# Moving gate products, a fourth sum and low parts from GpSimd to VectorE in a four-layer diffusion trunk

## The chip, the cores and the metric

The kernel runs on one core of a Trainium2 chip. Its engines run side by side, each through its own queue in order: TensorE (PE, and PEld for its weight loads) multiplies matrices into PSUM, VectorE (DVE) and ScalarE (ACT) read PSUM and SBUF, GpSimd (POOL) reads SBUF, and SyncE (SP) issues transfers. The metric is the time of one execution on the device in microseconds (us); the median of several executions counts.

## What is computed

Two layers of a trunk are applied to two groups of tokens, 128 of a context and 512 of a noisy latent. Each layer has three sub-layers: a SwiGLU, a mixer (a recurrent one in the first layer, a pooling one in the second) and another SwiGLU. All have the same frame, cut here to what matters:

```python
def _layer(x, mod, l, norm_g, ffn_w1, ffn_w3, ffn_w2, mixer):
    sh1, sc1, g1, sh2, sc2, g2, sh3, sc3, g3 = jnp.split(mod[:, None, :].astype(x.dtype), N_MOD, axis=-1)
    h = _modulate(_rmsnorm(x, norm_g[l, 0]), sh1, sc1)
    x = x + 0.5 * g1 * _rmsnorm(_swiglu(h, ffn_w1[l, 0], ffn_w3[l, 0], ffn_w2[l, 0]), norm_g[l, 1])
    h = _modulate(_rmsnorm(x, norm_g[l, 2]), sh2, sc2)
    y, st = mixer(h)
    x = x + g2 * _rmsnorm(y, norm_g[l, 3])
    h = _modulate(_rmsnorm(x, norm_g[l, 4]), sh3, sc3)
    x = x + 0.5 * g3 * _rmsnorm(_swiglu(h, ffn_w1[l, 1], ffn_w3[l, 1], ffn_w2[l, 1]), norm_g[l, 5])
    return x, st
```

with `_swiglu(x, w1, w3, w2) = (silu(x @ w1) * (x @ w3)) @ w2`, 1024 channels and 2816 hidden ones, all in float32.

## The kernel before

The 640 tokens lie as five tiles of 128: 0 to 3 are the latent, 4 is the context. A float32 operand of a product is split into a high part (a copy to a narrower type, on ScalarE) and a low part (the difference, a subtraction, on VectorE); three products of the parts give one (`split`, lines 218 to 220; the weights in `weight_gen`, L137 and L138, L178 and L181). The first matrices of a SwiGLU are multiplied by a scheme with seven products in place of eight: from the four quarters of the operand (A11, A12, A21, A22) it makes the sums S1 to S4 (`h_sums`), and the products take A11, A12, S2, S3, S1, A22 and S4 in that order, each with high and low part.

Where one sub-layer ends and the next begins, the kernel does the following for each of the five tiles (`close`):

- The last product of the old sub-layer is added to y, in two halves of 512 channels, n = 0 and 1 (L643, on VectorE, from PSUM; L1087 and L1089 after the pooling mixer).
- `res_half`: ScalarE sums the squares of the half (L385), and the half is then multiplied in place by the gate row G (L411), on VectorE for n = 1 of tiles 0 to 2 and on GpSimd for the rest. The product overwrites what the square reads, so it waits for it.
- `res_close`: VectorE adds up the squares (L379), GpSimd takes the power -1/2 (L381), and VectorE makes the residual x + y * power, in two halves (L419). `c_next` squares x on ScalarE, spills x through SP, takes another L379 and L381, and scales x on ScalarE (L431).
- `c_t`: TensorE transposes the scaled x (L505), ScalarE and VectorE apply the modulation to the transposed pieces (L516, L514). Ahead of the recurrent and the pooling mixer the result is split as it is (L219 high, L220 low). Ahead of a SwiGLU it feeds the quarters: tiles 0, 1 and half of tile 2 make A11 and A12, the other half of tile 2 and tiles 3 and 4 make A21 and A22, and with them the sums.
- `h_sums`: S1 (L464), S2 (L465), S3 (L468) on VectorE; S4 (L472) and the low part of A22 on GpSimd, named by `aside`; all high parts on ScalarE. Tile 2's halves of A11 and A12 are copied for later sums by GpSimd (L531).

There are six such places, which the text calls seams: after the first SwiGLU (to the recurrent mixer; around 475 to 530 us of the span), after the recurrent mixer (738 to 815), after the second SwiGLU (1200 to 1265), after the third (to the pooling mixer; 1678 to 1725), after the pooling mixer (1725 to 1815), and the end (2200 on), where x goes out instead of on. The sums are made after the second, third and fifth seam.

The order of TensorE's instructions is the program's own in most phases (`manual_schedule`); on the other engines a scheduler orders the instructions by priorities and by its own costs before the program runs, and that order is then fixed. Weights are loaded by SP, split some products ahead into a ring of buffers, and so their splits (L137, L138, L154 to L160, L178, L181) lie between the instructions of a seam.

Of the kernel before, what the change touches and what calls it, by code (L numbers as in the profile page):

```python
# [12 lines left out]
AF = mybir.ActivationFunctionType  # L13
ALU = mybir.AluOpType
# [19 lines left out]
HK = KC // 2  # L34
# [49 lines left out]
class Kern:  # L84
# [321 lines left out]
    def res_half(self, t, n, l, s):  # L406

        y = self.y[t][:, n * 512:(n + 1) * 512]
        v = 1 if t < NT - 1 else 0
        self.square(self.t("mhl", [P, 512], BF16), y, self.ms[t], n)  # L410
        (self.nc.vector if n and t < 3 else self.nc.gpsimd).tensor_tensor(y, y, self.G[(l, s)][:, v, n * 512:(n + 1) * 512], op=ALU.mult)  # L411

    def res_close(self, t):

# [60 lines left out]
    def c_t(self, tiles, l, s, plain, tag="q"):  # L475

        nc = self.nc
        ab = self.ab[(l, s)]
        t = tiles[0]
        v = 1 if t < NT - 1 else 0  # L480
        w = P * len(tiles)
        n = 512 // w
        sl = slice(t * P, t * P + w)
        second = None
        if not plain:
            if t * P + w <= HT:
                dst = lambda kk: self.F[0][kk // HK][:, kk % HK, sl]
            else:
                o = max(0, t * P - HT)
                sums = slice(o, (t + 1) * P - HT)  # L490
                if t * P < HT:
                    self.f2 = [self.view(self.t("g", [P, 2 * TOK])) for _ in range(4)]
                    hf = self.t("yacc", [P, D]).rearrange("p (k t) -> p k t", k=KC)
                    dst = lambda kk: hf[:, kk]
                    cut = HT - t * P
                    second = [hf[:, 0:HK, cut:P], hf[:, HK:KC, cut:P]] + [x[:, :, sums] for x in self.f2[2:]]
                else:
                    dst = lambda kk: self.f2[kk // HK][:, kk % HK, sums]
                    second = [x[:, :, sums] for x in self.f2]
                self.sums[t] = self.h_sums(slice(0, HK), sums, second, nc.gpsimd)  # L500
        for j in range(KC // n):
            pt = self.p(tag)
            for q in range(n):
                for i, tt in enumerate(tiles):
                    nc.tensor.transpose(pt[:, q * w + i * P:q * w + (i + 1) * P], self.y[tt][:, (j * n + q) * P:(j * n + q + 1) * P],  # L505
                                        self.col("ident"))
            if plain:
                hp = self.t("c", [P, n, w])
                dst = lambda kk: hp[:, kk % n]
            for q in range(n):  # L510
                kk = j * n + q
                sr = pt[:, q * w:(q + 1) * w]
                if j % 2:
                    nc.vector.tensor_scalar(dst(kk), sr, ab[:, 1, kk, v:v + 1], ab[:, 0, kk, v:v + 1], op0=ALU.mult, op1=ALU.add)  # L514
                else:
                    nc.scalar.activation(dst(kk), sr, AF.Identity, scale=ab[:, 1, kk, v:v + 1], bias=ab[:, 0, kk, v:v + 1])  # L516
            if plain:
                for q in range(0, n, 2):
                    k2 = (j * n + q) // 2
                    self.split(self.hh[k2][:, :, sl], self.hl[k2][:, :, sl], hp[:, q:q + 2])  # L520
        if plain:
            return
        if second is None:
            for j in range(2):
                self.h_first(j, slice(0, HK), sl)
        elif t * P < HT:
            own = slice(t * P, HT)
            for j, name in enumerate(("A11", "A12")):
                self.h_put(name, slice(0, HK), own, hf[:, j * HK:(j + 1) * HK, 0:cut])
            for j in range(2):  # L530
                nc.gpsimd.tensor_copy(self.F[0][j][:, :, own], hf[:, j * HK:(j + 1) * HK, 0:cut])  # L531


    def mmP(self, out, h, w, ks=range(HK), start=True, stop=True, first=0, last=HK - 1, onto=False):
# [837 lines left out]
```

## Time and profile before

| what | value |
|---|---|
| median of 3 runs | 2235.13 us (2234.14 to 2235.29) |
| profiled execution, its own time | 2239.17 us |
| its span in the trace | 2237.3 us |
| mean granted TensorE clock | 0.969 of full speed |
| busy: TensorE, VectorE, ScalarE, GpSimd | 2113.8, 1687.4, 1005.0, 169.3 us |

The profiled execution is one further execution, so times of the trace are counted against 2239.17 us and only differences are carried to the median. Starts in the trace are counted in us from the beginning of its span.

### The profile page before, as it was taken

The page shows a single profiled execution, that of the slowest core. Times are in us where ns is not written, and L with a number is a line of the kernel's source. Part 1 is how long each engine was busy: PE and PEld are TensorE (multiplying, and loading weights), DVE is VectorE, ACT ScalarE, POOL GpSimd, SP SyncE. Part 2 cuts the span into 40 slices and gives each one's busy share as a digit, 9 for nine tenths or more (in the row PEclk, how much of TensorE's full clock was granted, in tenths as well). Part 3 has the DMA queues.
Part 4 walks back from the last instruction along what each step waited for, and adds up shares of the span by engine and source line. Part 5 has one row for each costly group of instructions (what it writes and reads, how often), then busy time and mean ns, then how long its engine had stood idle before and what let it go on. Part 6 is the DMA issues. An engine that isn't in the chain of part 4 may idle for free.

```text
span 2237.3 us, 32900 instructions
## 1 busy us (share of the span) xinstructions
PE 2113.8 (94%) x13101; PEld 1916.7 (86%) x13101; DVE 1687.4 (75%) x2647; ACT 1005.0 (45%) x1733; POOL 169.3 (8%) x173
## 2 busy tenths in 40 slices
PE   6899999998898989999999899999997789999997
PEld 4798999987797778999998798988996779999997
DVE  5967777767978796777877977777776786787875
ACT  5443333357857654333335542332336754333332
POOL 0000000012201310000002200000002320000002
PEclk7999999998999999999999999999998989999999
DMA  8424422234424453432224434444434352222222
GB/s 278 169 99 151 151 76 95 76 113 132 137 95 151 151 177 104 153 130 73 86 76 151 170 110 144 152 152 146 155 104 142 112 185 85 76 94 75 77 75 94
DMA packets 72714, 278.26 MB, mean 124 GB/s; under 512 B 7393, under 2 KB 15601, under 8 KB 61297
## 3 DMA queue, kind: packets, MB, share of 16 engines
q1 hardware_dynamic: 72528, 276.16, 35.9%
q8 instruction: 102, 1.67, 0.3%
q14 instruction: 52, 0.42, 0.1%
q0 software_dynamic: 32, 0.01, 0.0%
HBM read 260.40 MB, written 15.74 MB: 123 GB/s over the span
## 4 chain that ended last, share of the span: by engine, by line
PE 78%; DVE 11%; ACT 5%; issue 2%; POOL 2%; DMA 2%; SPq 1%; POOLq 0%; DVEq 0%; ACTq 0%
PE q L540 40%; PE b L633 25%; PE b L540 6%; PE m L287 2%; PE q L549 2%; DVE h L220 2%; DVE mw L419 2%; POOL st L381 1%; DVE wp L138 1%; ACT yacc L431 1%; DMA raw<-in_w_dram 1%; DVE st L379 1%; DVE wp L181 1%; DVE h L926 1%; PE b L887 1%
## 5 line engine op out<-in xcount | busy, mean ns | idle before, releaser
L540 PE MATMUL q<-h,wp 128*128 128x320 f32 x6312 | 946.0, 311 | 15.1 <-ACT h L219 8.9
L540 PEld LDWEIGHTS q<-h,wp 128*128 128x128 f32 x6312 | 933.6, 189 | 30.5 <-ACT h L219 10.4
L633 PE MATMUL b<-wp,g 128*128 128x512 f32 x2880 | 672.0, 393 | 4.6 <-DVE g L220 2.6
L633 PEld LDWEIGHTS b<-wp,g 128*128 128x128 f32 x2880 | 540.4, 189 | 124.4 <-DVE g L220 4.3
L137 ACT ACTIVATE wp<-raw 128x512 fp32r<-128x512 f32 x430 | 263.1, 629 | 631.1 <-PE b L633 328.0
L643 DVE TENSOR_TENSOR yacc<-yacc,b 128x512 f32<-128x512 f32 x380 | 258.1, 685 | 140.4 <-PE b L633 139.3
L138 DVE TENSOR_TENSOR wp<-raw,wp 128x512 fp32r<-128x512 f32 x430 | 294.4, 692 | 82.8 <-ACT wp L137 80.7
L181 DVE TENSOR_TENSOR wp<-raw,wp 128x1024 fp32r<-128x1024 f32 x118 | 144.1, 1222 | 77.8 <-PE q L540 52.5
L540 PE MATMUL b<-h,wp 128*128 128x320 f32 x960 | 156.7, 322 | 24.9 <-ACT h L219 16.8
L540 PEld LDWEIGHTS b<-h,wp 128*128 128x128 f32 x960 | 147.5, 196 | 36.1 <-ACT h L219 18.8
L178 ACT ACTIVATE wp<-raw 128x1024 fp32r<-128x1024 f32 x94 | 99.6, 1059 | 162.4 <-PE q L540 143.8
L411 POOL TENSOR_TENSOR yacc<-yacc,G 128x512 f32<-128x512 f32 x42 | 58.6, 1401 | 1320.7 <-ACT mhl L385 1320.5
L137 ACT ACTIVATE wp<-T 128x512 fp32r<-128x512 f32 x176 | 105.1, 623 | 70.6 <-PE q L540 70.6
L154 DVE TENSOR_TENSOR T<-raw 128x1024 f32<-128x1024 f32 x88 | 107.6, 1223 | 37.9 <-DMA raw<-in_w_dram 36.8
L549 PE MATMUL q<-h,wp 128*128 128x320 f32 x768 | 123.5, 316 | 8.9 <-ACT h L219 6.6
L549 PEld LDWEIGHTS q<-h,wp 128*128 128x128 f32 x768 | 117.1, 193 | 13.2 <-ACT h L219 6.9
L138 DVE TENSOR_TENSOR wp<-T,wp 128x512 fp32r<-128x512 f32 x176 | 116.7, 687 | 10.3 <-ACT wp L137 10.0
L287 PE MATMUL m<-mw,csil 128*32 128x256 f32 x1024 | 72.6, 393 | 9.1 <-DMA mw<-in_mod_w_dram 9.1
L219 ACT ACTIVATE g<-c 128x1280 fp32r<-128x1280 f32 x44 | 56.2, 1278 | 43.1 <-DVE c L615 42.9
L220 DVE TENSOR_TENSOR g<-c,g 128x1280 fp32r<-128x1280 f32 x44 | 65.4, 1486 | 11.2 <-ACT g L219 11.1
L609 ACT ACTIVATE c<-c 128x960 f32<-128x960 f32 x44 | 44.0, 1000 | 47.3 <-DVE c L586 47.3
L160 DVE TENSOR_TENSOR raw<-raw 128x512 f32<-128x512 f32 x88 | 60.4, 686 | 1.1
(211 smaller groups left out, 1736.7 us busy)
## 6 DMA issues: line engine op xcount, KB each, us to landing
raw<-in_w_dram SPq DMA_DIRECT2D x88, 1024.0 KB, 4.8
mw<-in_mod_w_dram SPq DMA_DIRECT2D x130, 512.0 KB, 4.5
raw<-in_w_dram SPq DMA_DIRECT2D x88, 512.0 KB, 4.6
x_spill<-mw SPq DMA_DIRECT2D x25, 512.0 KB, 2.6
mw<-x_spill SPq DMA_DIRECT2D x25, 512.0 KB, 3.7
raw<-in_w_dram SPq DMA_DIRECT2D x32, 256.0 KB, 5.5
raw<-in_w_in_dram SPq DMA_DIRECT2D x16, 512.0 KB, 4.4
wp<-in_mod_w_dram SPq DMA_DIRECT2D x8, 512.0 KB, 9.7
```

The costliest lines, as they stand in the source:

```text
L137: parts = [nc.scalar.activation(w[:, 0:512], src, AF.Copy), V.tensor_sub(w[:, 512:D], src, w[:, 0:512].bitcast(F32))]
L138: V.tensor_sub(w[:, 512:D], src, w[:, 0:512].bitcast(F32))]
L154: V.tensor_sub(T, raw[:, 512:1536], raw[:, 0:1024])
L160: V.tensor_sub(t4, t2, b21)
L178: nc.scalar.activation(wh, r, AF.Copy)
L181: V.tensor_sub(wl, r, wh.bitcast(F32))
L220: (engine or self.nc.vector).tensor_tensor(lo, src, hi.bitcast(F32), op=ALU.subtract))
L287: nc.tensor.matmul(ps[32 * j:32 * j + 32, 0:256], self.csil[:, k, :], w[:, j * 256:(j + 1) * 256], start=(k == 0), stop=(k == KC - 1), til ...
L540: self.nc.tensor.matmul(out, a, b[:, k], start=(start and not onto and k == first and n == 0), stop=(stop and k == last and n == 2), skip_ ...
L549: self.nc.tensor.matmul(out, a[:, sl], b[k // 2][:, k % 2, cols], start=(n == 0), stop=(n == 3 * KC - 1))
L633: nc.tensor.matmul(pb, a[:, ts_], b[:, ns], start=(c == 0), stop=(c == total - 1))
L643: nc.vector.tensor_add(y, y, pb)
```

## The change

Three lines change. In `res_half` the gate products stay on GpSimd only for n = 0 of tiles 0 and 1; before, GpSimd had n = 0 of all tiles and n = 1 of tiles 3 and 4. So 12 of the 60 products of the program are left on GpSimd, where there were 42. In `c_t` the sums are made without `aside`, so that S4 and the low part of A22 go to VectorE, and the two copies of tile 2 go to ScalarE.

```diff
@@ -408,7 +408,7 @@
         y = self.y[t][:, n * 512:(n + 1) * 512]
         v = 1 if t < NT - 1 else 0
         self.square(self.t("mhl", [P, 512], BF16), y, self.ms[t], n)
-        (self.nc.vector if n and t < 3 else self.nc.gpsimd).tensor_tensor(y, y, self.G[(l, s)][:, v, n * 512:(n + 1) * 512], op=ALU.mult)
+        (self.nc.vector if n or t > 1 else self.nc.gpsimd).tensor_tensor(y, y, self.G[(l, s)][:, v, n * 512:(n + 1) * 512], op=ALU.mult)
 
     def res_close(self, t):
 
@@ -497,7 +497,7 @@
                 else:
                     dst = lambda kk: self.f2[kk // HK][:, kk % HK, sums]
                     second = [x[:, :, sums] for x in self.f2]
-                self.sums[t] = self.h_sums(slice(0, HK), sums, second, nc.gpsimd)
+                self.sums[t] = self.h_sums(slice(0, HK), sums, second)
         for j in range(KC // n):
             pt = self.p(tag)
             for q in range(n):
@@ -528,7 +528,7 @@
             for j, name in enumerate(("A11", "A12")):
                 self.h_put(name, slice(0, HK), own, hf[:, j * HK:(j + 1) * HK, 0:cut])
             for j in range(2):
-                nc.gpsimd.tensor_copy(self.F[0][j][:, :, own], hf[:, j * HK:(j + 1) * HK, 0:cut])
+                nc.scalar.activation(self.F[0][j][:, :, own], hf[:, j * HK:(j + 1) * HK, 0:cut], AF.Copy)
```

The scheduler also orders VectorE's and ScalarE's instructions anew around the moved ones. Three places on VectorE show it.

The first is the end of the sums of the third seam, from tile 4's S2 on, before the change. `h_11016` is the low part of S2, `h_11018` of S3, `h_11020` of S1 and `h_11022` of S4; `wp` are weights of later products.

```order
L220 TENSOR_TENSOR h_11020<-g_11298,h_11019 128x4x128
L220 TENSOR_TENSOR h_11022<-c_11026,h_11021 128x4x128
L220 TENSOR_TENSOR h_11016<-g_11299,h_11015 128x4x128
L468 TENSOR_TENSOR c_11025<-c_11025,g_11296 128x4x128
L220 TENSOR_TENSOR h_11020<-g_11298,h_11019 128x4x128
L220 TENSOR_TENSOR h_11022<-c_11026,h_11021 128x4x128
L220 TENSOR_TENSOR h_11018<-c_11025,h_11017 128x4x128
L138 TENSOR_TENSOR wp_11576<-T_11570,wp_11576 128x512
```

The same place of the changed program, on the same engine, with `h_11024` for the low part of A22 and `c_11026` for S4:

```order
L220 TENSOR_TENSOR h_11016<-g_11299,h_11015 128x4x128
L220 TENSOR_TENSOR h_11024<-g_11297,h_11023 128x4x128
L472 TENSOR_TENSOR c_11026<-c_11026,g_11299 128x4x128
L468 TENSOR_TENSOR c_11025<-c_11025,g_11296 128x4x128
L220 TENSOR_TENSOR h_11020<-g_11298,h_11019 128x4x128
L220 TENSOR_TENSOR h_11022<-c_11026,h_11021 128x4x128
L220 TENSOR_TENSOR h_11018<-c_11025,h_11017 128x4x128
L220 TENSOR_TENSOR h_11024<-g_11297,h_11023 128x4x128
L472 TENSOR_TENSOR c_11026<-c_11026,g_11299 128x4x128
L156 TENSOR_TENSOR raw_11331<-raw_11331,T_11570 128x512
L573 TENSOR_TENSOR c_11553<-b_11555,yacc_11325 128x320
L220 TENSOR_TENSOR h_11022<-c_11026,h_11021 128x4x128
```

L472 and A22's low parts now stand between VectorE's own instructions; S2's last low part has five instructions between it and S3's last where it had three, and S4's last comes after all others.

The second place is tile 3 in the first seam (`yacc_1085` is its y, `yacc_1086` tile 4's, `mw_4436` its x).

```order
 L220 TENSOR_TENSOR h_4349<-c_4543,h_4345 128x2x256
 L643 TENSOR_TENSOR yacc_1086<-yacc_1086,b_4579 128x512
+L411 TENSOR_TENSOR yacc_1085<-yacc_1085,G_1435 128x512 x2
+L379 SCALAR_TENSOR_TENSOR st_4489<-st_4489 128x1
 L220 TENSOR_TENSOR h_4350<-c_4553,h_4346 128x2x256
-L379 SCALAR_TENSOR_TENSOR st_4489<-st_4489 128x1
-L181 TENSOR_TENSOR wp_4660<-raw_4216,wp_4315 128x1024
 L419 SCALAR_TENSOR_TENSOR mw_4436<-yacc_1085,st_4525,mw_4436 128x512 x2
 L220 TENSOR_TENSOR h_4351<-c_4563,h_4347 128x2x256
```

Both products of tile 3 now stand one behind the other in VectorE's queue, with the sum of squares behind them, and the weight split L181 that stood ahead of the residual has gone further back.

The third place is the end of the program (`yacc_17055`, `yacc_17056` and `yacc_17057` are y of tiles 2, 3 and 4).

```order
+L411 TENSOR_TENSOR yacc_17056<-yacc_17056,G_17275 128x512
 L643 TENSOR_TENSOR yacc_17056<-yacc_17056,b_20321 128x512
+L411 TENSOR_TENSOR yacc_17056<-yacc_17056,G_17275 128x512
 L379 SCALAR_TENSOR_TENSOR st_20303<-st_20303 128x1
+L643 TENSOR_TENSOR yacc_17057<-yacc_17057,b_20345 128x512
 L419 SCALAR_TENSOR_TENSOR mw_20258<-yacc_17056,st_20339,mw_20258 128x512 x2
-L643 TENSOR_TENSOR yacc_17057<-yacc_17057,b_20345 128x512
+L411 TENSOR_TENSOR yacc_17057<-yacc_17057,G_17275 128x512
 L643 TENSOR_TENSOR yacc_17057<-yacc_17057,b_20362 128x512
+L411 TENSOR_TENSOR yacc_17057<-yacc_17057,G_17275 128x512
 L379 SCALAR_TENSOR_TENSOR st_20344<-st_20344 128x1
 L419 SCALAR_TENSOR_TENSOR mw_20301<-yacc_17057,st_20380,mw_20301 128x512 x2
```

Each half is now added, multiplied, and only then is the next half added, and tile 4's first add has moved ahead of tile 3's residual.

## Rows read from the trace of the kernel before

**Rows 1.** The page: busy time by engine, and TensorE's 40 slices in tenths.
```profile
PE 2113.8 (94%) x13101; PEld 1916.7 (86%) x13101; DVE 1687.4 (75%) x2647; ACT 1005.0 (45%) x1733; POOL 169.3 (8%) x173
...
PE   6899999998898989999999899999997789999997
```

**Rows 2.** Five seams: stretch, length, busy PE, PEld, DVE, ACT, POOL; clock, DMA.
```profile
470.00:530.00 60.00, 49.06 (x245) 41.70 (x244) 42.23 (x76) 37.09 (x88) 17.80 (x20) 0.89 0.42 140
735.00:815.00 80.00, 70.62 (x418) 61.08 (x417) 66.58 (x113) 50.74 (x112) 26.02 (x26) 0.94 0.43 150
1195.00:1265.00 70.00, 56.75 (x320) 49.56 (x319) 62.43 (x100) 46.19 (x106) 27.99 (x25) 0.93 0.39 136
1675.00:1725.00 50.00, 39.13 (x210) 33.92 (x210) 32.45 (x57) 31.78 (x76) 16.25 (x17) 0.90 0.49 158
1725.00:1815.00 90.00, 68.20 (x405) 62.58 (x406) 66.40 (x119) 61.87 (x145) 33.58 (x25) 0.84 0.32 106
```

**Rows 3.** Timeline of TensorE: start, duration, instructions, idle time before and its releaser.
```profile
509.08 0.90 PE L549 MATMUL q<-h,wp 128*128 128x320 f32 x2 [6.62 <-ACT h L219]
...
797.82 5.39 PE L540 MATMUL b<-h,wp 128*128 128x320 f32 x35 [0.73 <-DVE h L220]
...
1253.62 0.64 PE L540 MATMUL b<-h,wp 128*128 128x320 f32 x1 [5.86 <-ACT h L219]
1257.24 8.42 PE L540 MATMUL b<-h,wp 128*128 128x320 f32 x47 [2.99 <-DVE h L220]
...
1811.06 8.21 PE L540 MATMUL b<-h,wp 128*128 128x320 f32 x36 [3.85 <-ACT h L219]
```

**Rows 4.** One line, the gate products L411: min/median/max in ns by engine.
```profile
L411 POOL TENSOR_TENSOR yacc<-yacc,G x42: 1262/1292/2123, 478.7 to 2230.3; 128x512 f32<-128x512 f32 x42
...
L411 DVE TENSOR_TENSOR yacc<-yacc,G x18: 678/686/1139, 480.6 to 2219.1; 128x512 f32<-128x512 f32 x18
```

**Rows 5.** Timelines of GpSimd and VectorE, first seam; then line L379 as in rows 4.
```profile
500.55 2.95 POOL L411 TENSOR_TENSOR yacc<-yacc,G 128x512 f32<-128x512 f32 x2 [2.06 <-ACT mhl L385]
...
502.30 1.23 DVE L379 SCALAR_TENSOR_TENSOR st<-st 128x1 f32<-128x1 f32 x1
...
505.10 1.41 DVE L419 SCALAR_TENSOR_TENSOR mw<-yacc,st,mw 128x512 f32<-128x512 f32 x2 [0.44 <-POOL st L381]
...
L379 DVE SCALAR_TENSOR_TENSOR st<-st x60: 139/159/1246, 7.2 to 2229.8; 128x1 f32<-128x1 f32 x60
```

**Rows 6.** Groups by form on VectorE, 1239.2 to 1259.6: count, busy us, mean ns, idle.
```profile
L465 DVE TENSOR_TENSOR g<-g,c 128x512 f32<-128x512 f32 x2 | 2.4, 1214 | 0.0
...
L468 DVE TENSOR_TENSOR c<-c,yacc 128x256 f32<-128x256 f32 x1 | 0.4, 412 | 0.0
```

**Rows 7.** Timeline of VectorE: tile 4's residuals (second, third, fifth seam) and third seam's sums.
```profile
774.01 1.41 DVE L419 SCALAR_TENSOR_TENSOR mw<-yacc,st,mw 128x512 f32<-128x512 f32 x2 [0.44 <-POOL st L381]
...
1237.91 1.41 DVE L419 SCALAR_TENSOR_TENSOR mw<-yacc,st,mw 128x512 f32<-128x512 f32 x2 [0.44 <-POOL st L381]
1239.24 1.04 DVE L514 TENSOR_SCALAR g<-b,ab 128x128 f32<-128x128 f32 x3
...
1258.32 1.28 DVE L220 TENSOR_TENSOR h<-c,h 128x512 fp32r<-128x512 f32 x2
...
1786.38 1.42 DVE L419 SCALAR_TENSOR_TENSOR mw<-yacc,st,mw 128x512 f32<-128x512 f32 x2 [1.24 <-POOL st L381]
```

**Rows 8.** Timeline of VectorE at the end: product, and residuals of tiles 1 and 4.
```profile
2213.38 0.69 DVE L411 TENSOR_TENSOR yacc<-yacc,G 128x512 f32<-128x512 f32 x1 [0.85 <-ACT mhl L385]
...
2214.88 1.41 DVE L419 SCALAR_TENSOR_TENSOR mw<-yacc,st,mw 128x512 f32<-128x512 f32 x2 [0.73 <-POOL st L381]
...
2232.14 1.42 DVE L419 SCALAR_TENSOR_TENSOR mw<-yacc,st,mw 128x512 f32<-128x512 f32 x2 [1.75 <-POOL st L381]
```

**Rows 9.** Timeline of GpSimd in the fifth seam; then the powers L381 as in rows 4.
```profile
1800.44 6.42 POOL L220 TENSOR_TENSOR h<-yacc,h 128x256 fp32r<-128x256 f32 x1 [4.30 <-ACT h L219]
...
L381 POOL TENSOR_TENSOR st<-st,mhalf x60: 543/549/2001, 7.6 to 2231.6; 128x1 f32<-128x1 f32 x60
```

## The prediction

> **What bounds the kernel now.** The page comes first: TensorE is busy for 94% of the span, and in its 40 slices it stands at 8 or 9 tenths nearly everywhere but at the start and where one sub-layer ends and the next begins [rows 1]. There are six such places (I call them seams), and they are what a change on the other engines can move. The table by stretch is next: in the five seams that are followed by more work TensorE does 39 to 71 us in stretches of 50 to 90 us, VectorE fills 62.4 of 70 us in the third, and GpSimd is busy for 16 to 34 us in each [rows 2]. What TensorE waits for stands in its timeline: after the third seam the product with S2 waits 5.86 us for ScalarE's high part and 2.99 us more for VectorE's low part; after the second and the fifth the product with S3 comes last, at 797.82 and 1811.06; in the first, the transposed tokens come at 509.08 after 6.62 us [rows 3]. All of these come out of one chain: gate product, power, residual, norm, transpose, sums, splits, and the end of it runs on VectorE.
>
> Then one looks at what GpSimd does to VectorE. A gate product takes 1.29 us on GpSimd and 0.69 us on VectorE [rows 4]. But GpSimd's are not free for VectorE: while two of them run from 500.55 to 503.50, a VectorE instruction on one column (L379) takes 1.23 us instead of its usual 0.16, and ends at 503.53 [rows 5]. In the third seam's sums two 512-wide subtractions (L465) average 1214 ns [rows 6], where such an instruction lasts 0.68 when nothing holds it [rows 7]. So VectorE stands still for most of a GpSimd instruction that it meets.
>
> The Trainium skill ("SBUF — State Buffer", section "SBUF: two separate sides") has this as an exclusive lock: a VectorE instruction with two SBUF inputs and a GpSimd instruction that reads SBUF block each other for a whole instruction. The trace agrees (503.53 against 503.50). If the two shared bandwidth in halves instead, what I credit to the sums below would be about halved, and the time would be near 2226 us, an estimate. The rule also speaks against the change, since the powers stay on GpSimd and now meet more VectorE instructions: that is the rival on the slow side, priced from rows.
>
> **The change, part by part.** *Products.* Five of ten products a seam go from GpSimd to VectorE (n = 0 of tile 2, both of tiles 3 and 4). When VectorE has work queued one costs a step of 0.60 us (two low parts take 1.28 with 0.68 each [rows 7]), so 3.0 us a seam. *Sums.* For each of three tiles in the second, third and fifth seam the fourth sum (L472) and the low part of A22 (L220) move too: per seam two instructions of 256 columns and four of 512, at steps of 0.33 (one lasts 0.41 [rows 6], and starts overlap by 0.08 as the 512-wide do) and 0.60: 3.1 us. *Copies.* Two copies of 256 columns a seam go to ScalarE, which has 24 to 29 us free in those seams [rows 2]; they stand ahead of other work in its queue, and by the 0.41 of VectorE I put them at 0.8 us on tile 2's chain at most. They are inside the waits below.
>
> *The sums phase of the second, third and fifth seam* carries the prediction. I measure from the end of tile 4's residual (its second L419) to the last low part of S3, and count in the new order what stands between.
> - Third: before 1239.32 to 1259.60 = 20.3 us [rows 7]. New: 7 transposed pieces (L514) x 0.32 (three take 1.04 [rows 7]) = 2.2, 9 instructions of 256 columns x 0.33 = 3.0, 15 of 512 x 0.60 = 9.0, one L379 0.1: 14.3 us. For waits on ScalarE's high parts I add 1.4 (a walk by hand through the new order finds one of 0.8 before the first split, and some of 0.2). The phase starts about 0.4 earlier: 20.3 - 14.3 - 1.4 + 0.4 = 5.0 us gained.
> - Second: before 775.42 [rows 7] to 797.82 [rows 3] = 22.4 us. New: 8 x 0.32 + 9 x 0.33 + 19 x 0.60 (four weight splits among them) + 0.1 = 17.0, waits 1.4; the start 1.0 earlier, since no pair of products on GpSimd holds tile 4's L379: 5.0 us.
> - Fifth: before 1787.80 [rows 7] to 1811.06 [rows 3] = 23.3 us, in which GpSimd's low part of A22 took 6.42 us [rows 9] and the fourth sum and TensorE waited behind it. New: 8 x 0.32 + 9 x 0.33 + 17 x 0.60 + 0.1 = 15.8, waits 2.1; the start 1.0 earlier: 6.4 us.
>
> TensorE is idle by then (in the third it has waited since 1247.8), so it gains what S3 gains. Sum: 16.4. Bounds: if the waits for ScalarE eat what is saved, 0 to 2 each; if the phases start as early as my walks allow and the clock falls less (granted 0.84 to 0.94 over these seams [rows 2]), 8 each. I stay near the count, as it is made of measured steps.
>
> *First and fourth seam.* Tile 3's pair ended at 503.50, and the L379 behind it let the residual start only at 505.10 [rows 5]. On VectorE each product waits for ScalarE's square; where nothing lies between, that wait is 0.85 us [rows 8]. The walk ends the second product at 502.7 and starts the residual at 503.5, 1.6 us earlier. One weight split (L181) that stood ahead now comes behind the residual, in front of tile 2's low parts, which takes back 0.6. I take 1.0 us for each of the two; bounds -1 (a loss) and 3 (tile 4's chain earlier too, if the loads leave TensorE work).
>
> *End.* Here nothing hides the in-order waits. From the end of tile 1's residual at 2216.29 [rows 8], new: tile 2: add 0.6, wait 0.85, product 0.6, add 0.6, wait 0.85, statistics and product beside the power 0.85, residual 1.4 = 5.75; tile 3, with its power behind the product, 6.4; tile 4, whose first add lies under tile 3's power, 4.9. That is 2233.3 against 2233.56: 0, bounds -1 and 1.
>
> Sum: 16.4 + 2.0 + 0 = 18.4 us. The profiled execution took 2239.2 us (span 2237.3), 4 above the median of 2235.1; taken off the profile it gives 2220.8, off the median 2216.7.
>
> Queues: no DMA is added; residual and spill shift by a microsecond or so between SP's weight loads. What is late next, should it work, are the weight splits: some that lay inside the sums now follow them, while TensorE resumes 5 us earlier. In the third seam the walk has the first one needed (wp_11573) ready 2 us before its product.
>
> **The rivals.**
> *Powers starve (slower).* L381 stays on GpSimd and gets in late while VectorE issues two-input instructions back to back: 2001 ns at worst, median 549 [rows 9]. The new order puts a product right behind some L379. About six powers a seam gate something, 36 in all; the gain of 18.4 is gone when each comes 0.5 us later. At 0.75 us: 27 lost, 2244 us. For it: GpSimd's 6.42 us [rows 9], when VectorE was never idle. Against: the median is the bare time, and where the residual is next in VectorE's own queue, VectorE stops and lets the power through.
> *VectorE's freed time is not TensorE's (same).* TensorE's first wait names ScalarE's h [rows 3]; if ScalarE, with the copies and its weight copies moved, sets the pace, only the fifth seam's stall goes: -3, 2232 us. Against: ScalarE is busy for 46 of 70 us there [rows 2].
> *Half of it.* The waits between VectorE and ScalarE are some 3 us a sums phase longer than I walk, as each split alternates between the two: -9, 2226 us.
> *More.* TensorE's idle stretches shrink, the clock falls less, and the first and fourth seam give 3 each: -26, 2209 us.
>
> **How the numbers follow.** The count as it stands (-13 to -23, so 2212 to 2222): 0.47. Half: 0.20. More: 0.13. Same: 0.12, its centre just inside the bound. Slower: 0.08. About 0.2% (4.5 us) is what a measurement tells from no change. Faster is the first three, 0.80. The range runs from 2207 to 2231: it leaves out the far part of "more" (0.03), most of "same" (0.09) and "slower" (0.08). I name 2217.
>
> **What would show it.** In the profile after: no L472, L220 or L531 on GpSimd; the L465 group of the sums near 0.68; S3's last low part some 5 us closer to tile 4's residual in three seams; tile 3's L419 of the first seam 1.6 us earlier; the long L379 gone outside tiles 0 and 1. It is wrong if L381's mean grows by over half a microsecond, if VectorE's idle time before splits (released by ScalarE) grows by what was saved, or if TensorE waits for weight splits just after the sums.

## The result, and the profile after

The changed kernel takes 2219.38 us (median of 4 runs, 2215.69 to 2221.05) where the kernel before took 2235.21 us beside it (4 runs, 2234.14 to 2237.29): a ratio of 0.9925 with a 95% interval of 0.9911 to 0.9938. It is faster by 15.8 us, counted by the medians. The profiled execution took 2221.05 us, its span is 2219.3 us, 18.0 us shorter than the span of before. 2217 was forecast, with 18.4 us to gain.

The page of the kernel after has this row, which answers to the first of [rows 1]:

```profile
PE 2110.4 (95%) x13101; PEld 1911.5 (86%) x13101; DVE 1683.0 (76%) x2695; ACT 1005.4 (45%) x1739; POOL 95.0 (4%) x119
```

VectorE has 48 instructions more than before and is busy for 4.4 us less. Moving the work away from GpSimd took 74 us off GpSimd and added nothing to VectorE's busy time: what it now does itself it used to spend inside instructions that were held up.

The table by stretch of the kernel after, at the same times as in [rows 2] (the later seams have moved up by 4 to 9 us inside their stretch; columns as there):

```profile
470.00:530.00 60.00, 52.69 (x283) 44.79 (x282) 43.43 (x83) 37.53 (x90) 9.14 (x15) 0.94 0.43 150
735.00:815.00 80.00, 71.36 (x445) 61.52 (x444) 70.72 (x133) 53.74 (x117) 9.90 (x13) 1.00 0.45 158
1195.00:1265.00 70.00, 61.15 (x355) 53.51 (x354) 59.38 (x114) 45.89 (x106) 12.73 (x12) 0.95 0.44 152
1675.00:1725.00 50.00, 37.35 (x201) 33.21 (x200) 32.03 (x65) 35.05 (x83) 7.19 (x10) 0.83 0.47 159
1725.00:1815.00 90.00, 78.79 (x522) 71.32 (x522) 76.41 (x146) 64.64 (x147) 11.86 (x12) 0.94 0.44 149
```

VectorE was already the fuller of the two engines, and in the second seam it is now busy for 70.7 of 80 us (66.6 before), GpSimd for 9.9 (26.0 before). The granted clock in the second seam rose from 0.94 to 1.00 of full speed and in the fifth from 0.84 to 0.94; in the fourth stretch it fell, from 0.90 to 0.83.

Where the time went is read from the start of the same instruction in both traces. The table takes a product L633 of TensorE that lies between one seam and the next (in the trace of before those at 735.2, 835.9, 1675.6 and 1851.5 us; behind the fourth seam L1079 at 1744.2) and gives what each seam adds to its shift, in us; minus is earlier. "Again" is a second trace of the same kernel, both against the first trace of before.

| seam | forecast | after | after, again | before, again |
|---|---|---|---|---|
| first | -1.0 | -4.3 | -4.8 | -0.5 |
| second | -5.0 | -2.9 | -2.6 | 0.0 |
| third | -5.0 | -1.0 | -1.1 | +1.4 |
| fourth | -1.0 | -1.0 | -2.2 | -1.4 |
| fifth | -6.4 | -9.5 | -8.4 | 0.0 |
| end | 0 | +0.5 | +0.5 | 0.0 |

(In the two traces of after the first seam begins 0.2 and 0.6 late, in that of before, again, 0.4 early.) The sum came out as forecast; the split over the seams did not. The last column shows how far one unchanged seam differs between two executions. At 735.2 the shift of after is just moving, from -4.7 at 730.5 to -3.7 at 736.8, so that half a microsecond or so could be counted to the second seam in place of the first.

TensorE's waits in the kernel after, as in [rows 3]:

```profile
507.55 0.63 PE L549 MATMUL q<-h,wp 128*128 128x320 f32 x1 [4.96 <-ACT h L219]
...
792.05 2.03 PE L540 MATMUL b<-h,wp 128*128 128x320 f32 x12 [0.48 <-DVE c L573]
...
795.46 5.92 PE L540 MATMUL b<-h,wp 128*128 128x320 f32 x36 [0.38 <-DVE c L577]
802.60 4.07 PE L540 MATMUL b<-h,wp 128*128 128x320 f32 x24 [1.22 <-DVE c L573]
...
1229.97 1.90 PE L505 MATMUL b<-cols,yacc 128*128 128x128 f32 x8 [2.39 <-ACT yacc L431]
1245.51 0.42 PE L540 MATMUL b<-h,wp 128*128 128x320 f32 x1 [0.36 <-ACT h L219]
1246.75 1.89 PE L540 MATMUL b<-h,wp 128*128 128x320 f32 x11 [0.82 <-DVE h L220]
...
1259.32 2.03 PE L540 MATMUL b<-h,wp 128*128 128x320 f32 x12 [0.59 <-DVE c L580]
1262.12 5.53 PE L540 MATMUL b<-h,wp 128*128 128x320 f32 x36 [0.77 <-DVE c L583]
...
1794.87 5.45 PE L540 MATMUL b<-h,wp 128*128 128x320 f32 x35 [0.38 <-DVE h L220]
```

In the third seam the waits of 5.86 and 2.99 us before the sums' products have become 0.36 and 0.82. Two things are new. TensorE waits 2.39 us for tile 3's scaled x, before the sums begin. And behind the sums it waits for VectorE's additions of the seven-product scheme (L580 and L583 in the third seam; L573, L577 and L573 again in the second), which no row of [rows 3] has. The group of sums that answers to [rows 6], from the kernel after between 1234 and 1251 (count, busy us, mean ns, idle):

```profile
L465 DVE TENSOR_TENSOR g<-g,c 128x512 f32<-128x512 f32 x2 | 1.4, 688 | 0.0
```

It took 1214 ns before.

### The profile page after: what moved, and what is told of

It reads as the page before. It is cut to its first block, busy times and chain, and to the rows that moved or that the text cites. A ratio compares the mean times of both kernels' runs of the same rounds, so it can differ in the third digit from the quotient of the medians.

```text
span 2219.3 us, 32870 instructions
## 1 busy us (share of the span) xinstructions
PE 2110.4 (95%) x13101; PEld 1911.5 (86%) x13101; DVE 1683.0 (76%) x2695; ACT 1005.4 (45%) x1739; POOL 95.0 (4%) x119
## 4 chain that ended last, share of the span: by engine, by line
PE 76%; DVE 12%; ACT 6%; issue 2%; DMA 2%; POOL 1%; SPq 1%; POOLq 0%; DVEq 0%; ACTq 0%
PE q L540 41%; PE b L633 25%; PE b L540 5%; PE m L287 2%; DVE h L220 2%; PE q L549 2%; POOL st L381 1%; DVE wp L138 1%; DVE mw L419 1%; ACT yacc L431 1%; DVE h L926 1%; ACT mhl L385 1%; PE b L887 1%; ACT yacc L385 1%; DVE yacc L411 1%
## 5 line engine op out<-in xcount | busy, mean ns | idle before, releaser
L633 PE MATMUL b<-wp,g 128*128 128x512 f32 x2880 | 671.7, 393 | 4.7 <-DVE g L220 2.7
L633 PEld LDWEIGHTS b<-wp,g 128*128 128x128 f32 x2880 | 540.2, 189 | 124.3 <-DVE g L220 4.4
L181 DVE TENSOR_TENSOR wp<-raw,wp 128x1024 fp32r<-128x1024 f32 x118 | 144.2, 1222 | 75.2 <-PE q L540 52.9
L540 PE MATMUL b<-h,wp 128*128 128x320 f32 x960 | 151.6, 313 | 13.8 <-DVE h L220 4.0
L540 PEld LDWEIGHTS b<-h,wp 128*128 128x128 f32 x960 | 141.2, 188 | 26.4 <-ACT h L219 5.6
L154 DVE TENSOR_TENSOR T<-raw 128x1024 f32<-128x1024 f32 x88 | 107.7, 1224 | 41.0 <-DMA raw<-in_w_dram 39.9
L220 DVE TENSOR_TENSOR g<-c,g 128x1280 fp32r<-128x1280 f32 x44 | 65.4, 1487 | 11.2 <-ACT g L219 11.1
L411 POOL TENSOR_TENSOR yacc<-yacc,G 128x512 f32<-128x512 f32 x12 | 16.1, 1345 | 1320.4 <-ACT mhl L385 1320.4
```

What stands on the lines that cost most here:

```text
L154: V.tensor_sub(T, raw[:, 512:1536], raw[:, 0:1024])
L181: V.tensor_sub(wl, r, wh.bitcast(F32))
L220: (engine or self.nc.vector).tensor_tensor(lo, src, hi.bitcast(F32), op=ALU.subtract))
L540: self.nc.tensor.matmul(out, a, b[:, k], start=(start and not onto and k == first and n == 0), stop=(stop and k == last and n == 2), skip_ ...
L633: nc.tensor.matmul(pb, a[:, ts_], b[:, ns], start=(c == 0), stop=(c == total - 1))
```

## The experiments

Every ratio is to the kernel before on the same chip, with its 95% interval; on this scale 0.001 is 2.2 us. The shifts by seam are made as in the table above.

**Products alone, and sums alone.** Two kernels each carry one line of the change.

```diff
# products alone
-        (self.nc.vector if n and t < 3 else self.nc.gpsimd).tensor_tensor(y, y, self.G[(l, s)][:, v, n * 512:(n + 1) * 512], op=ALU.mult)
+        (self.nc.vector if n or t > 1 else self.nc.gpsimd).tensor_tensor(y, y, self.G[(l, s)][:, v, n * 512:(n + 1) * 512], op=ALU.mult)
# sums alone
-                self.sums[t] = self.h_sums(slice(0, HK), sums, second, nc.gpsimd)
+                self.sums[t] = self.h_sums(slice(0, HK), sums, second)
```

> Only the gate products' line is changed; sums and copies stay as before. The count of the prediction: first and fourth seam as in the full change (there, 3.8 and 0.9 us by the shift of the same instructions between the two traces), and in the other three only the earlier start of the sums phase (0.4 to 1.0 us each): 6 to 7.5 us in all, near 2228. Rival (the sums' locks on GpSimd fill what the products free): only the first and fourth seam gain, 4.7 us, 2230.5. Rival (powers starve behind VectorE's added products): third seam worse than before, total gain under 2 us, 2233 or more.

Measured: 0.9978 (0.9968 to 0.9988), 2231.4 us, 5 us faster than before. By seam, first to fifth: -4.2, +2.0, +2.4, -4.5, -3.3. The count's total (6 to 7.5) was missed by little, but its split is wrong: the second and third seam become worse. The rivals each have a piece of it: the first and fourth seam gain, and the third loses, though not enough to turn the whole. The trace shows what the second seam lost. A22's low part was still on GpSimd here, and took 5.82 us where it had taken 0.74 before; the fourth sum (L472) stood behind it in GpSimd's queue, and ScalarE waited 4.79 us for that sum (GpSimd, then ScalarE):

```profile
781.09 5.82 POOL L220 TENSOR_TENSOR h<-yacc,h 128x256 fp32r<-128x256 f32 x1 [4.91 <-ACT h L219]
```
```profile
789.38 1.15 ACT L219 ACTIVATE h<-c 128x512 fp32r<-128x512 f32 x2 [4.79 <-POOL c L472]
```

TensorE then waited 3.32 us for ScalarE. It still began the products with S3 6.0 us earlier than before, 0.8 of it gained in this seam, but came out of the wait at the lower clock (granted 0.66 from 790 to 800, where it was 1.00 from 797 to 803 before), and 35 products took 7.99 us in place of the 5.39 of [rows 3]:

```profile
791.78 7.99 PE L540 MATMUL b<-h,wp 128*128 128x320 f32 x35 [0.69 <-DVE h L220]
```

In the third seam the same low part took 5.03 us. So with the sums left on GpSimd, moving the products made the stall of the fifth seam in [rows 9] (6.42 us) appear in the second and the third as well.

> Only the fourth sum and A22's low part go to VectorE; products and copies stay as before. The count: first, fourth seam and end unchanged within 0.3 us; second, third and fifth gain what is left of 5.0, 5.0 and 6.4 without the earlier starts (4.0, 4.6, 5.4), 14 us, 2221. What the trace of the full change suggests instead: the third seam's small gain (1.0) is owed to a power that came 2.4 us late behind VectorE's products, so that here, with the products on GpSimd, the third seam should gain 3 to 4.5. Rival (the third seam is set by ScalarE's high parts or by weight splits after it): it gains 1 here too, and the total is 8 to 11 us, 2224 to 2227.

Measured: 0.9936 (0.9923 to 0.995), 2223.3 us, 14 us faster than before: the count's 14. By seam: -2.6, -1.5, -3.7, -1.7, -6.6. The third seam gains 3.7 here and 1.0 in the full change, as expected if the products cost it something. In this kernel the order of the first seam is that of before, instruction by instruction, and still the trace is 2.6 us shorter there. A window of it, and then the same one of before, show where a part of that came from:

```profile
560.00:590.00 30.00, 28.25 (x201) 27.34 (x201) 28.73 (x41) 28.18 (x42) 5.45 (x9) 1.00 0.44 150
```
```profile
560.00:590.00 30.00, 28.24 (x192) 27.42 (x191) 27.45 (x38) 26.70 (x41) 5.13 (x8) 0.94 0.43 148
```

TensorE was granted the higher of its two levels (2.4 GHz) all the time from 560 to 590 here, and the lower one for a part of it there, and got 9 more matmuls done. The second trace of before has 0.94 and 192 matmuls there again, so that this is not shown to be chance between executions; why this kernel was granted more is open. One seam can thus be 2 to 3 us off between two kernels that have the same order in it, and only larger differences, or those that a row explains, are read below.

**The same two kernels again**, for the spread.

> The kernel before, once more, for a second trace. The first trace's execution took 2239.2 us against a median of 2235.1, and in the run with only the sums moved the first and the fourth seam, where nothing of consequence was changed, were 2.5 and 1.6 us shorter than in that trace. If the first trace had a bad first and fourth seam by chance, this one has its first seam 2 to 2.5 us shorter (TensorE's work after it starts that much earlier), and a span near 2233. If those seams are really shortened by moving the sums, it has them as the first trace, and the span is near 2237.

Its span was 2236.5 us, and the first seam 0.5 us shorter: neither forecast is met fully, but the first trace of before was no odd one. Its clock and its matmuls from 560 to 590 are those of the first trace, so the shorter first seam of the kernel with sums alone stays a difference between two kernels, of which the clock shows a part and the cause is open.

> The full change, once more, beside the others of this call and for a second trace: ratio 0.9925 as measured. By seam (shift of the same instructions against the first trace of after): under 0.5 us everywhere if its seams are steady, and if the third seam's late power (3.20 us at 1225.96) is a matter of order and not of chance, it is there again within 0.1 us.

Measured: 0.9923 (0.991 to 0.9935). The late power is there again, 3.20 us. The fourth and fifth seam differ by 1.2 and 1.1 between the two traces, more than I expected, the others by 0.6 or less.

**The late power.** Timelines of GpSimd, VectorE and ScalarE of the kernel after, third seam:

```profile
1225.96 3.20 POOL L381 TENSOR_TENSOR st<-st,mhalf 128x1 f32<-128x1 f32 x1 [2.87 <-DVE st L379]
```
```profile
1225.66 0.16 DVE L379 SCALAR_TENSOR_TENSOR st<-st 128x1 f32<-128x1 f32 x1
1225.73 1.29 DVE L138 TENSOR_TENSOR wp<-raw,wp 128x512 fp32r<-128x512 f32 x2
1226.94 0.69 DVE L411 TENSOR_TENSOR yacc<-yacc,G 128x512 f32<-128x512 f32 x1
1227.54 1.22 DVE L154 TENSOR_TENSOR T<-raw 128x1024 f32<-128x1024 f32 x1
1231.18 0.69 DVE L411 TENSOR_TENSOR yacc<-yacc,G 128x512 f32<-128x512 f32 x1 [2.42 <-ACT mhl L385]
```
```profile
1229.20 1.33 ACT L431 ACTIVATE yacc<-mw,st 128x512 f32<-128x512 f32 x2 [2.96 <-POOL st L381]
```

The power of tile 3's second norm is asked for at 1225.82, when L379 ends. Four two-input instructions follow on VectorE without a gap until 1228.76, and only 0.4 us after that, at 1229.16, is the power done (0.55 us is the bare time). ScalarE waits 2.96 us for it, TensorE 2.39 us, and VectorE itself stands still for 2.42 us, since tile 4's second square is queued on ScalarE behind the scaling. This is the prediction's rival "powers starve", in one place. One kernel lets the power through: VectorE gets a one-column copy that reads it, and so has to stop (the edit is cut to that line).

```diff
         rs = self.rstd(ms)
+        with self.tc.high_priority(2000): self.nc.vector.tensor_copy(self.t("st", [P, 1]), rs)
```

> The full change, and in the second half of each tile's work (the norm of the next sub-layer) VectorE gets a one-column copy that reads the power, with high priority: in its order it stands one or two instructions behind the statistics, so that VectorE has to stop until GpSimd's power is through. It computes nothing that is used. If the third seam loses 2.4 us because VectorE's back-to-back instructions keep the power out, the power there takes 1.0 to 1.4 us in place of 3.2, and the seam gains 1.5 to 2.5 us; the 25 stops cost VectorE 0.6 us each, hidden where TensorE is not waiting: 0 to 2 us faster than the full change, 2217 to 2219. Rival (the late power is not what TensorE waits for in the end, since VectorE catches up on weights meanwhile): the power is short and the third seam gains nothing; the stops make the whole 2 to 6 us slower.

Measured: 0.9934 (0.992 to 0.9948), against 0.9923 of the full change beside it: not faster, perhaps a little slower. By seam: -2.9, -0.1, -2.0, -1.5, -11.2. The power is short now:

```profile
1232.14 0.86 POOL L381 TENSOR_TENSOR st<-st,mhalf 128x1 f32<-128x1 f32 x1 [3.47 <-DVE st L379]
```

It ends 2.3 us sooner after its request, but the third seam gains only 1.0 more than in the full change, not 2.4. Its request came at 1232.1, 6.2 us later than in the full change, of which 4.6 was lost before this seam and 1.6 in it. That the stops had made VectorE late, and so took what the power won, is the likely reading and not shown. The second seam, whose powers had been punctual, lost 2.5 to 2.8 us beside the full change, and the first 1.4 to 1.9.

**No products on GpSimd at all, and both together.**

```diff
-        (self.nc.vector if n or t > 1 else self.nc.gpsimd).tensor_tensor(y, y, self.G[(l, s)][:, v, n * 512:(n + 1) * 512], op=ALU.mult)
+        self.nc.vector.tensor_tensor(y, y, self.G[(l, s)][:, v, n * 512:(n + 1) * 512], op=ALU.mult)
```

> The full change, and the last twelve products (n = 0 of tiles 0 and 1) go to VectorE too, so that GpSimd keeps nothing in the seams but powers. If a GpSimd product holds VectorE for its length, as the rows of before had it, VectorE gets back 12 x (1.29 - 0.60) = 8 us, but early in each seam, where TensorE still has the old sub-layer's products: 0 to 4 us faster than the full change, 2215 to 2219. Rival (the in-order wait for ScalarE's square costs VectorE more than the lock): 2 to 5 us slower than the full change, 2221 to 2224.

Measured: 0.9919 (0.9906 to 0.9933), 2218.3 us. The interval overlaps that of the full change; if it is better, then by a microsecond. By seam: -4.1, -2.8, -1.9, -1.6, -9.5.

> All sixty gate products on VectorE, and the one-column copy that lets the power through only in the third and the fifth seam, where the kernel that has it everywhere gained (2.0 and 11.2 us against the first trace of before, where the full change gained 1.0 and 8.5 to 9.5). If the two effects are independent, this is 2 to 3 us faster than the kernel with all products on VectorE: ratio 0.991, near 2215 on the scale of 2235. If the copy's gain in the fifth seam was the clock's chance and the third's is what all products on VectorE had already got (1.9), it is the same as that kernel, 0.992.

Measured: 0.9919 (0.9906 to 0.9933), the same as without the copy. No power in the third seam's second half is over 1 us any more (2.60 us without the copy), and the seam gains 2.0, as with all products alone: the second of the two expectations. So making the power short did not by itself gain anything in this seam. Tile 4's residual starts no earlier for it. The rows are the power of tile 3 and the residual of tile 4 in this kernel, and that residual in the kernel with the copy in every seam:

```profile
1227.86 0.86 POOL L381 TENSOR_TENSOR st<-st,mhalf 128x1 f32<-128x1 f32 x1 [3.47 <-DVE st L379]
```
```profile
1233.12 1.41 DVE L419 SCALAR_TENSOR_TENSOR mw<-yacc,st,mw 128x512 f32<-128x512 f32 x2 [0.34 <-POOL st L381]
```
```profile
1237.56 1.42 DVE L419 SCALAR_TENSOR_TENSOR mw<-yacc,st,mw 128x512 f32<-128x512 f32 x2 [0.34 <-POOL st L381]
```

Beside what the seams ahead had gained, they end 1.6 and 2.0 us late; in the full change, with the power at 3.20 us, it was 1.8.

**The copies.** Products and sums are moved, tile 2's two copies stay on GpSimd.

```diff
-                nc.scalar.activation(self.F[0][j][:, :, own], hf[:, j * HK:(j + 1) * HK, 0:cut], AF.Copy)
+                nc.gpsimd.tensor_copy(self.F[0][j][:, :, own], hf[:, j * HK:(j + 1) * HK, 0:cut])
```

> The full change, but tile 2's two copies go back to GpSimd: products and sums are moved, copies are not. Two instructions of 128x256 a seam on GpSimd, in reach of VectorE's residual of tile 3. If they lock VectorE as the products did, 0.5 to 1 us a seam are lost in three seams: 2 to 3 us slower than the full change, 2221 to 2223 on the scale of 2235. If ScalarE's copies delay tile 2's and tile 3's chain instead (rival), it is 1 to 2 us faster, 2217 to 2218.

Measured: 0.9929 (0.9916 to 0.9941) beside 0.9923 of the full change: no difference that can be told, with its median 1.2 us higher. The copies are a small part of the change, if any.

**What one instruction costs on either engine.** The low part of A22 is made twice, the second time with the same result, on VectorE in one kernel (`V`, shown here) and on GpSimd in the other (`self.nc.gpsimd` in its place).

```diff
-        self.h_put("A22", ks, cols, f22, aside)
+        self.h_put("A22", ks, cols, f22, aside); V.tensor_tensor(self.H["A22"][1][:, ks, cols], f22, self.H["A22"][0][:, ks, cols], op=ALU.subtract)
```

> The full change, and the low part of A22 is made a second time, on VectorE, with the same result. It adds one instruction of 256 columns and two of 512 in each of the three sums phases (and two of 640 at the program's start). By the steps of the prediction (0.33 and 0.60) that is 1.5 us a seam; what lies before S3's last low part delays TensorE by as much, what lies behind it does not. 2 to 4.5 us slower than the full change: 2221 to 2224 on the scale of 2235. If VectorE is not what the sums phase waits for, under 1 us.

Measured: 0.9959 (0.9946 to 0.9973), 0.0035 or some 8 us above the full change; its profiled span is 3.7 us longer. By seam against the first trace of after: -2.1, +1.7, +2.9, -2.4, +2.4. The three seams with sums lose 7.0 us where the added instructions take 4.6; the first and the fourth, to which nothing was added, came out 2 us shorter, so the 7.0 is uncertain by as much. More than the 2 to 4.5 us expected, and far from the 1 us of the other reading: VectorE is what the sums phases wait for.

> As the last, but the second copy of A22's low part is made on GpSimd, which has nothing else to do there: the same elements, once on VectorE's account and once on GpSimd's. If a GpSimd instruction that reads SBUF holds VectorE for its length (1.29 us for 512 columns, 0.66 for 256), 3.2 us a seam are lost on VectorE although it does no more work than in the full change: 5 to 9 us slower than the full change, 2224 to 2229, and VectorE instructions of over 1.2 us lie beside it in the trace. If they share bandwidth in halves, 2 to 4.5 us. If GpSimd does not hold VectorE at all, none, and the gain of the full change must have come from elsewhere (order, clock).

Measured: 0.9968 (0.9956 to 0.9981), 10 us above the full change, and not cheaper than the same work on VectorE. GpSimd and VectorE in the third seam of this kernel:

```profile
1247.93 8.62 POOL L471 TENSOR_TENSOR h<-yacc,h 128x256 fp32r<-128x256 f32 x1 [7.04 <-DVE h L220]
1256.51 3.41 POOL L471 TENSOR_TENSOR h<-g,h 128x512 fp32r<-128x512 f32 x2
```
```profile
1255.86 0.50 DVE L573 TENSOR_TENSOR c<-b,yacc 128x320 f32<-128x320 f32 x1
1256.26 0.84 DVE L220 TENSOR_TENSOR h<-c,h 128x512 fp32r<-128x512 f32 x1
1257.03 1.77 DVE L138 TENSOR_TENSOR wp<-raw,wp 128x512 fp32r<-128x512 f32 x1
1258.72 2.35 DVE L138 TENSOR_TENSOR wp<-T,wp 128x512 fp32r<-128x512 f32 x2
```

Both directions are in these rows. From 1247.70 to 1255.86 VectorE issues fourteen instructions with two inputs in SBUF, without a gap, and GpSimd's 256 columns wait through all but the first; they end at 1256.55, 0.7 us after the start of L573, the first in that row with an input in PSUM (b). Then GpSimd has its turns, and a 512-wide VectorE instruction takes 1.77 us in place of 0.69: a GpSimd instruction of 512 columns costs VectorE 1.08 us. Neither forecast of the lock covers both halves: GpSimd holds VectorE, but here only once it has got in. The lateness has a price of its own: TensorE waits 1.98 us for the low part itself, so the 10 us are not VectorE's loss alone. And GpSimd does not always wait that long. In the fifth seam of the same kernel 512 columns got in between two VectorE instructions of the same kind, without a gap (TensorE in the third seam; GpSimd and VectorE in the fifth):

```profile
1259.97 2.58 PE L540 MATMUL b<-h,wp 128*128 128x320 f32 x11 [1.98 <-POOL h L471]
```
```profile
1796.65 1.59 POOL L471 TENSOR_TENSOR h<-g,h 128x512 fp32r<-128x512 f32 x1 [3.59 <-DVE h L220]
```
```profile
1796.43 0.68 DVE L472 TENSOR_TENSOR c<-c,g 128x512 f32<-128x512 f32 x1
1797.03 1.76 DVE L220 TENSOR_TENSOR h<-g,h 128x512 fp32r<-128x512 f32 x1
```

**Less work for VectorE.** All products on VectorE, and the modulated pieces that VectorE makes of tile 4 (in the second kernel those of tiles 2 to 4, with `t < 2`) go to ScalarE.

```diff
-                if j % 2:
+                if j % 2 and t < 4:
```

> All gate products on VectorE as before, and tile 4's four modulated pieces that VectorE makes (0.33 us each in a row) go to ScalarE, in all seams (their ScalarE form takes 0.45). In the full change VectorE runs without a gap from tile 4's residual until well behind the sums, and TensorE then waits for its adds; if VectorE is what holds TensorE there, 1.3 us less of its work gives 0.8 to 1.3 us in the second, third and fifth seam: 2 to 4 us faster than with all products alone, ratio 0.990 to 0.991. Rival (ScalarE, busy for 15.4 of 22 us in the third seam's sums, sets the pace with its high parts, which now come behind these pieces): 1 to 4 us slower, 0.9925 to 0.9935.

Measured: 0.9922 (0.991 to 0.9935): no gain. 

> The same for tiles 2, 3 and 4: 3.9 us a seam less on VectorE, about 4.5 more on ScalarE. If VectorE is the bound, 2 to 3 us a seam in three seams, 5 to 8 us faster than with all products alone: 0.988 to 0.990. If ScalarE takes over as the bound of the sums phase (its 46 to 63 us of 70 to 90 grow by 4.5 a seam), it gains no more than with tile 4 alone, or loses: 0.991 to 0.994.

Measured: 0.9953 (0.994 to 0.9967), 7.5 us slower than with all products alone. In the third seam of the first of these two kernels TensorE no longer waits for VectorE's additions, but the product with S2 comes 2.9 us later than with all products alone, 0.9 more than the seams ahead had lost; in the second kernel it waits for ScalarE again:

```profile
1246.28 0.41 PE L540 MATMUL b<-h,wp 128*128 128x320 f32 x1 [0.90 <-ACT h L219]
```
```profile
1246.09 0.64 PE L540 MATMUL b<-h,wp 128*128 128x320 f32 x1 [2.63 <-ACT h L219]
```

So VectorE and ScalarE are nearly in balance after the change: shifting the pieces of one tile gains nothing, those of three tip it. No version measured here beats the full change by more than its interval. For the powers on VectorE itself there is no measurement.

## Why the prediction held, step by step

**The sums on VectorE carry the gain: right.** Alone they give 14 us of the 16 to 17. What GpSimd had held is visible in the sums' group, 1214 to 688 ns. The rule of the Trainium skill that the prediction weighed ("SBUF — State Buffer", section "SBUF: two separate sides", an exclusive lock and not a split of bandwidth) agrees with 1.77 against 0.69 us for a VectorE instruction beside GpSimd's. A split in halves, priced at 2226 us, does not fit: by the prediction's working it would have about halved the gains of 4.0, 4.6 and 5.4 us that were counted for the phases, which came out at 4.8, 4.1 and 4.1.

**The sums phases: the count was right, the ends around it were not.** From tile 4's residual to S3's last low part, with the kernel after's rows of VectorE:

```profile
768.87 1.42 DVE L419 SCALAR_TENSOR_TENSOR mw<-yacc,st,mw 128x512 f32<-128x512 f32 x2 [0.44 <-POOL st L381]
...
786.59 1.29 DVE L220 TENSOR_TENSOR h<-c,h 128x512 fp32r<-128x512 f32 x2
787.79 0.69 DVE L220 TENSOR_TENSOR h<-g,h 128x512 fp32r<-128x512 f32 x1
788.39 0.69 DVE L472 TENSOR_TENSOR c<-c,g 128x512 f32<-128x512 f32 x1
...
789.19 1.20 DVE L154 TENSOR_TENSOR T<-raw 128x1024 f32<-128x1024 f32 x1
790.32 0.67 DVE L220 TENSOR_TENSOR h<-c,h 128x512 fp32r<-128x512 f32 x1
790.93 0.67 DVE L156 TENSOR_TENSOR raw<-raw,T 128x512 f32<-128x512 f32 x1
791.53 0.47 DVE L573 TENSOR_TENSOR c<-b,yacc 128x320 f32<-128x320 f32 x1
...
1232.67 1.42 DVE L419 SCALAR_TENSOR_TENSOR mw<-yacc,st,mw 128x512 f32<-128x512 f32 x2 [0.35 <-POOL st L381]
...
1249.01 1.30 DVE L220 TENSOR_TENSOR h<-c,h 128x512 fp32r<-128x512 f32 x2
...
1774.30 1.41 DVE L419 SCALAR_TENSOR_TENSOR mw<-yacc,st,mw 128x512 f32<-128x512 f32 x2 [1.24 <-POOL st L381]
```

The first addition behind the second phase in the kernel before, and the powers of the kernel after as in [rows 9]:

```profile
798.49 0.47 DVE L573 TENSOR_TENSOR c<-b,yacc 128x320 f32<-128x320 f32 x1
```
```profile
L381 POOL TENSOR_TENSOR st<-st,mhalf x60: 543/548/3202, 7.7 to 2213.6; 128x1 f32<-128x1 f32 x60
```

Each seam splits into three parts: how much earlier tile 4's residual ends (beside what the seams ahead had gained), the phase from there to S3, and what follows.

| seam | start: forecast, measured | phase: forecast, measured | behind it: forecast, measured |
|---|---|---|---|
| second | -1.0, -1.0 | -4.0, -4.8 | 0, +2.9 |
| third | -0.4, +1.8 | -4.6, -4.1 | 0, +1.3 |
| fifth | -1.0, -3.2 | -5.4, -4.1 | 0, -2.2 |

For the third: the residual ends at 1234.09, 5.2 us before the 1239.32 of [rows 7], where 7.0 had been gained already, so it starts 1.8 late; the low part ends at 1250.31, after 16.2 us where 20.3 were needed; TensorE's shift falls from -9.3 there to -8.0 in the end. The fifth is counted to TensorE's start at 1794.87, as in [rows 3].

The middle column, the one made of counted steps (0.32, 0.33, 0.60 us), is within 1.3 us in each seam. The mis-sized terms are the other two:

- *Third seam, start: -0.4 forecast, +1.8 measured.* The late start goes with the products: tile 4's residual is 1.7 us late with products alone and on time with sums alone. "Powers starve" was a rival with 0.5 us for each of 36 powers; in fact the typical power stayed as it was (median 548 ns against 549), and one took 3.20 us. In the rows of the third seam above it delays ScalarE, TensorE and tile 4's second square. But that this power is the cause is not shown: in the two kernels that make it short, the residual starts as late. What the moved products cost there, beside it, stays open.
- *Behind the second and third phase: 0 forecast, +2.9 and +1.3 measured.* "What is late next are the weight splits" named the right place and gave it no price. The rows from 787.79 on show it for the second seam: between S3's last low part and VectorE's first addition (L573) stand the moved low part of A22, the moved L472, a weight split's sum L154, the low part of S4 and L156, 3.65 us where 0.7 passed before (797.8 to 798.49). TensorE waits 0.48, 0.38 and 1.22 us for those additions, and 0.59 and 0.77 us in the third seam. The kernel that makes A22's low part twice on VectorE adds work ahead of S3 as well as here, so it does not price this place alone.
- *Behind the fifth: 0 forecast, -2.2 measured.* Before, TensorE came out of its wait of 3.85 us at the lower clock: 36 products took 8.21 us [rows 3], at a granted 0.70 from 1811 to 1820; now 35 take 5.45, at 1.00 from 1794 to 1800. That is the rival "more", in one seam.

**First seam, 1.0 forecast with a bound of 3; 4.3 and 4.8 measured.** Tile 3's residual starts at 503.58, 1.5 us earlier than [rows 5] (1.6 forecast), and TensorE's first product with it. The rest is tile 4, which I put down only as a bound. In TensorE's timeline, before and after, its transposes:

```profile
521.06 1.76 PE L505 MATMUL b<-cols,yacc 128*128 128x128 f32 x7 [3.34 <-ACT yacc L431]
```
```profile
517.57 0.44 PE L505 MATMUL b<-cols,yacc 128*128 128x128 f32 x2 [0.60 <-ACT yacc L431]
```

They came 3.5 us earlier. Of this, 1.45 is the 2.00 us power of [rows 9]: it stood at 518.25 before, beside two weight splits on VectorE, and the new order has taken it out of their way (0.55 us at 516.21). The other 2.0 is its earlier start. So the change made one power late and another one punctual. What makes up the remaining 0.8 to 1.3 us is not shown.

**Fourth seam and end.** 1.0 forecast, 1.0 and 2.2 measured; at the end 0 forecast, 0.5 lost. Both right within the spread; the two traces of the unchanged kernel differ by 1.4 in the fourth seam, so that a gain there is not told from none. The errors of the third and second seam (4.0 and 2.1 too much) and of the first and fifth (3.3 and 3.1 too little) cancel. That the total came out 0.4 us from the forecast is luck: it was better than its parts.

Open stays how much of the fifth seam's 9.5 us is the earlier start of tile 4's residual by itself, and how much the clock; the traces show both and no run separates them. Open too is why the third seam starts late with the products on VectorE.

## What to carry to other kernels

An instruction on GpSimd beside a busy VectorE is not spare capacity: price it as if VectorE did the work, and move it only if it lies where VectorE is idle. When the phase in question is shortened on the engine that bounds it, look at what that engine does directly behind the phase, since moved work comes out there; and look at every GpSimd instruction that is left and that someone waits for, and what VectorE has queued in the microseconds behind its request. Moving one kind of work alone can make what is left wait longer, as the products alone did. A forecast by stage should be compared by stage: here a good total hid four terms that were off by 2 to 4 us.

## What the runs showed of the hardware

- GpSimd can wait long beside VectorE instructions that follow each other without a gap and read two inputs from SBUF. A 128x256 subtraction took 8.62 us in one kernel and 5.82 in another, where the kernel before had 0.74; a 128x1 power took 3.20 where 0.55 was usual. All three ended within 0.7 us of the first gap, or of the first VectorE instruction with an input in PSUM. It is no rule without exception: a 128x512 subtraction got in between two such VectorE instructions and was done in 1.59 us. Which of the two happens, no run here settles.
- Once GpSimd had got in, the next two GpSimd instructions got in too, at 1.08 us of VectorE's time for each 512 columns (1.77 us in place of 0.69).
- The granted clock of TensorE from 560 to 590 was 0.94 in both traces of the kernel before and 1.00 in that of the kernel with sums alone, which has the same order in this seam. The seam was 2.6 us shorter; the cause is open.
